# Router logits on four column tiles, a 128-column first gather, filler products and a new order of early expert loads in a two-layer decoder trunk

## The chip, the cores and the metric

The kernel runs on one core of one Trainium2 chip. The metric is the device time of one execution in microseconds; the median of three runs stands for it. Traces come from one profiled execution. The engines are called PE (matrix products, with PEld its weight loads), DVE (vector), ACT (scalar and activation), POOL and SP (whose queue issues nearly all loads here).

## The reference, cut to what matters

Two layers of a decoder trunk over 256 tokens of width 1024, all in float32. Each layer is an attention-like mixer followed by a channel mixer, each with RMSNorm before and after. The channel mixer of the second layer is a mixture of 8 experts, of which each token uses 2:

```python
logits = h @ w_router + b_router            # (256, 8)
probs = softmax(logits); top_p, top_e = top_k(probs, 2)
...
y = swiglu(rows, w_gate[e], w_up[e], w_down[e])   # 1024 -> 3584 -> 1024, per expert
out = segment_sum(y[dest] * sorted_w[:, None], sorted_tok)
```

The three matrices of an expert are 44 MB, those of all eight 352 MB; they are read once from HBM. The change lies at the border between the mixer of the second layer and these experts.

## The kernel before, in words

**Mixer, end of layer 1.** `mixer` ends with `wout(0, ...)`: products with `w_out` (L195 to L197, each float32 product as three of rounded parts) into accumulators, for token tile t = 0 and then t = 1 (128 tokens each). `update` scales, squares and adds the result to `self.x` (L401, L402, L408) and `measure` squares the new `x` (L245).

**Router logits.** `scorer` makes `ws` (router weights times the norm's scale, 8 columns for each of 8 slices of 128 channels). Its `score(t, after)` runs for t = 0 inside the update of t = 1 (behind an `Exp` on ACT) and for t = 1 after it. For each half of 512 channels it turns four 128x128 blocks of `x` on PE (L853, bank tag "s"), copies them to `xT` (L856 by ACT for t = 0; L858 by ACT and L859 by DVE, half each, for t = 1) and multiplies with the turned block as the weights and `ws` as 8 moving columns (L862): 8 products for each t.

**Routing.** `route` finishes the logits (L876), picks two experts per token by comparisons on DVE (L880 to L887), counts places with two products (L891, L892), and leaves `weights` for later. `places` makes the 0/1 matrix `pmr` (L1119), and `gather` multiplies `x` by it (L1139: 16 products of `x` blocks as weights with 64 moving columns for the first expert, which the profile counts as 32 instructions), scales the result (L1144 DVE, L1146 ACT), and the first expert's gate products (L1041) follow.

**Experts.** They run in a fixed order; four take 64 rows ("few": L1041, float32, two column tiles of 64) and four 128 rows (three products of rounded parts, L195 to L197, with conversions L179 on ACT and L180 on DVE). Expert 0 of the order is always the first one of the model, so its weights can be loaded before the routing is known. All weights are cut in units of 1 MB (42 per expert, 336 in all), loaded in the order of use by the generator `stream`; `take` hands them out.

**Where the early units go.** The first 18 units have a written `plan` of buffers: `None` is one of 6 rotating buffers `raw`, shared with the mixer's own loads and outside the expert pool; "g", "y", "f", "t4" are tiles of later use, taken as two halves of 512 KB; "a8" is one tag with 8 buffers of 1 MB. From unit 18 on, a `ring` of 15 buffers is used over again. SP's queue takes its issues in order; an issue whose buffer is still in use blocks those behind it. `behind` fixes the order of issue on one engine, and is no wait for the end of the other instruction.

The expert pool opens where the mixer's pools lay. Worked out from the shapes in the code, per partition and in order of address: "g" and "y" (8 KB each) lie on constants of the mixer and its `bias`; "f", "t4" on `os`, `on` and the rest of tag "h8"; then the eight 8 KB buffers, called a0 to a7 here: a0 on the tag "t2" (`xT` among it), a1 on its last buffer, `vv` and half of `kT`, a2 on `kT`, `qT`, `qn`, a3 on `qn`, `ks`, `vs`, `gr`, `gs`, a4 on small tiles and `sbe`, a5 on `sbe` and `sqs`, a6 on `sqs`, `gm` and `ws`, a7 beyond everything of the mixer of layer 1.

Of the kernel before, what the change touches and what calls it, by code (L numbers as in the profile page):

```python
# [9 lines left out]
F32 = mybir.dt.float32  # L10
# [5 lines left out]
OP = mybir.AluOpType  # L16
# [4 lines left out]
P = 128  # L21
D = 1024
S = 256
L = 2
KT = D // P
FF = 2816
FE = 3584
E = 8
EPS = 1e-6
BIG = 1e30  # L30
U = 2048
# [29 lines left out]
class Kernel:  # L61
# [6 lines left out]
    def run(self):  # L68
        tc, nc = self.tc, self.nc
        with ExitStack() as ctx:  # L70
            pool = lambda n, b, **k: ctx.enter_context(tc.tile_pool(name=n, bufs=b, **k))
            self.const = pool("const", 1)
            self.small = pool("small", 2)
            self.raw = pool("raw", RAW)
            self.hl = pool("hl", 4)
            self.psum = pool("psum", 2, space=PSUM)
            self.dr = pool("dr", 1, space=DRAM)
            with tc.tile_pool(name="mixers", bufs=1, reuse_waits="tile") as self.mix:
                with tc.tile_pool(name="set", bufs=1, reuse_waits="tile") as st:
# [746 lines left out]
    def level(self, l):  # L826
# [8 lines left out]
        nc.vector.tensor_tensor(level, pc[:, 0:E], self.brow, op=OP.add)  # L835
        return level

    def scorer(self, l, ph, ss, level):

        nc = self.nc  # L840
        wr = self.sm[:, SM_WR:SM_WR + 64].rearrange("p (k e) -> p k e", k=8)
        ws = ph.tile([P, KT, E], F32, name="ws")
        nc.vector.tensor_tensor(ws, wr, ss[:, :, None].to_broadcast([P, KT, E]), op=OP.mult)
        logits = []

        def score(t, after):
            pl = self.bank("t", "logits")
            logits.append(pl)
            for h in range(2):
                p = self.bank("s", "xT").rearrange("p (k t) -> p k t", k=4)  # L850
                xT = ph.tile([P, 4, P], F32, name="xT", tag="t2")
                for i in range(4):
                    nc.tensor.transpose(p[:, i], self.x[:, t, P * (4 * h + i):P * (4 * h + i) + P], self.ident)  # L853
                with self.behind(*after):
                    if t == 0:
                        nc.scalar.activation(xT, p, AF.Copy)  # L856
                    else:
                        nc.scalar.activation(xT[:, 0:2], p[:, 0:2], AF.Copy)  # L858
                        nc.vector.tensor_copy(xT[:, 2:4], p[:, 2:4])  # L859
                for i in range(4):  # L860
                    k = 4 * h + i
                    nc.tensor.matmul(pl[:, 0:E], lhsT=xT[:, i], rhs=ws[:, k], start=k == 0, stop=k == KT - 1)  # L862

        self.scores = logits, level
        return score

    def route(self, ph, gt, eq):


        nc = self.nc  # L870
        new = lambda n, *s: ph.tile([P, 2, *s], F32, name=n)
        pr, wt, pos, sel, scl = (new(n, E) for n in ("pr", "wt", "pos", "sel", "scl"))
        logits, level = self.scores
# [11 lines left out]
        selb = ph.tile([P, 2 * E], BF16, name="selb")  # L885
# [3 lines left out]
            nc.vector.tensor_scalar(scl[:, t], sel[:, t], r, None, op0=OP.mult)  # L889
        pp = self.bank("o", "places")  # L890
        nc.tensor.matmul(pp[:, 0:2 * E], lhsT=self.before, rhs=selb, start=True, stop=False, skip_group_check=True)  # L891
        nc.tensor.matmul(pp[:, E:2 * E], lhsT=self.one, rhs=selb[:, 0:E], start=False, stop=True, skip_group_check=True)  # L892
        nc.vector.tensor_copy(pos, pp[:, 0:2 * E].rearrange("p (t e) -> p t e", t=2))

        def weights():
# [52 lines left out]
    def moe(self, l, ph):  # L948
        tc, nc = self.tc, self.nc
        nch = FE // 512  # L950
        made = {}
# [2 lines left out]

        def tiles(tag):

            return made.get(tag) or [ph.tile([P, U // 2], F32, name="unit", tag=tag) for h in range(2)]

        def stream():

            last = ()
            plan = [None, None, None, "g", None, None, None, "y", "f", "t4", "a8", "a8", "a8", "a8", "a8", "a8", "a8", "a8"]
            ring = [t for t in plan if t in (None, "t4", "a8")]
            turn = 0
            for i, (name, p, u) in enumerate(units):
                tag = plan[i] if i < len(plan) else ring[(i - len(plan)) % len(ring)]
                if p == 0:
                    src = self.ins[name][FIRST, u]
                else:
                    if p > turn:  # L970
                        turn = p
                        expert.append(nc.values_load(turni[0:1, rank[p]:rank[p] + 1], engines=[ET.SP], min_val=0, max_val=E - 1))
                    src = self.ins[name][bass.ds(expert[p], 1), u].rearrange("o p f -> (o p) f")
                if tag is None:
                    yield self.load(src, after=last if i >= len(plan) else ())
                    if i > len(plan):
                        last = self.loaded,
                elif tag == "a8":
                    unit = ph.tile([P, U], F32, name="unit", tag=tag)
                    with self.behind(*(last if i >= len(plan) else ())):  # L980
                        self.loaded = nc.sync.dma_start(unit, src).ins
                    last = self.loaded,
                    yield unit
                else:
                    src = src.rearrange("p (h f) -> h p f", h=2)
                    unit = tiles(tag)
                    with self.behind(*(last if i >= len(plan) else ())):
                        for h, t in enumerate(unit):
                            self.loaded = nc.sync.dma_start(t, src[h]).ins
                    last = self.loaded,  # L990
                    yield unit
# [9 lines left out]
        ahead = [next(fetch) for i in range(4)]  # L1001
# [5 lines left out]
        made["f"] = tiles("f")  # L1007
        made["t4"] = tiles("t4")
        gm = ph.tile([P, D], F32, name="gm")
        ahead += [next(fetch) for i in range(14)]  # L1010
        made.clear()
        ss, sh = self.ffn_in
        wt, pos, sel, scl, weights = self.route(ph, gt, eq)

# [107 lines left out]
        def gather(e, pm, pmr, tags="t", xf=None):  # L1122

            few = short[e]
            n = 64 if few else P
            if few:
                xf = xf or ph.tile([P, KT, 64], F32, name="xf", bufs=2)
            else:
                xgh, xgl = [ph.tile([P, KT, P], F32R, name=n, tag="x4") for n in ("xgh", "xgl")]
            for h in range(2):  # L1130
                p = self.bank(tags[h % len(tags)], "gather").rearrange("p (a s) -> p a s", a=4)
                if not few:
                    xg = ph.tile([P, 4, P], F32, name="xg", tag="t2")
                else:
                    xg = xf[:, 4 * h:4 * h + 4]
                for a in range(4):
                    k = 4 * h + a
                    for t in range(2):
                        nc.tensor.matmul(p[:, a, 0:n], lhsT=self.x[:, t, P * k:P * k + P], rhs=pmr[:, t, 0:n],  # L1139
                                         start=a == 0 and t == 0, stop=t == 1, skip_group_check=True)  # L1140
# [52 lines left out]
        f, begun = [], None  # L1193
        for e in range(E):
# [3 lines left out]
            for c in range(nch):  # L1198
                pp = []
# [219 lines left out]
```

## Time and profile before

| what | value |
|---|---|
| median of 3 runs | 1452.79 us (1452.57 to 1456.24) |
| profiled execution, time | 1452.78 us |
| profiled execution, span | 1451.0 us, mean granted clock 0.968 |
| PE, DVE, ACT busy | 95%, 67%, 53% of the span |
| read from HBM | 479.87 MB, 332 GB/s over the span |
| DMA from 600 us on | about 420 GB/s until 1225 us |

The profiled execution's time is 1.8 us over its span, and as good as equal to the median, so sums can be made against it. Times in the rows below are microseconds from the start of the span. In the view by windows the numbers are the stretch, its length, the busy time (and count of instructions) of PE, PEld, DVE, ACT and POOL, the clock granted to PE as a share of full speed, the DMA share and GB/s. In the chain, each row is a start, a duration and the work that the end of the program goes back to. A busy PE is not one at its peak: records of products overlap, and their own durations (0.39 us for 512 columns) are longer than their distance (0.21 to 0.23 us).

### The profile page before, as it was taken

The numbers are of one execution on the slowest core, as the hardware profiler recorded it, in microseconds if no ns is written. First come the engines' busy times: TensorE is split into PE (matmuls) and PEld (weight loads), VectorE is DVE, ScalarE is ACT, GpSimd is POOL, SyncE is SP. The second block draws the span as 40 slices with busy tenths as digits, with TensorE's granted clock in tenths as the row PEclk, the third lists the DMA queues.
The fourth block names the chain that finished last, engine by engine and source line by source line (L and its number), as shares of the span: only waits on it lengthen the run. The fifth ranks groups of instructions, "written<-read, shape, count | busy, mean of one in ns | idle before, by whom it ended". The sixth has DMA issues, their size and how long they took to land.

```text
span 1451.0 us, 20370 instructions
## 1 busy us (share of the span) xinstructions
PE 1379.9 (95%) x7470; PEld 988.8 (68%) x7470; DVE 977.9 (67%) x1566; ACT 770.0 (53%) x1179; POOL 16.5 (1%) x24
## 2 busy tenths in 40 slices
PE   5899969999979999999999999999999999999996
PEld 5767759999877687544788534887435888788432
DVE  7678888877565774522999424998315989999413
ACT  3464654444554556232787324787324778787322
POOL 0100010000100000000000000000000000000000
PEclk9989979999979999799999999999999999999998
DMA  9936829888435284899999999999999999999994
GB/s 365 326 143 210 337 82 344 316 309 315 176 119 203 88 319 132 353 400 420 419 421 420 419 419 420 420 420 421 418 421 420 420 420 407 345 368 375 369 421 182
DMA packets 73479, 482.52 MB, mean 333 GB/s; under 512 B 10315, under 2 KB 10484, under 8 KB 18588
## 3 DMA queue, kind: packets, MB, share of 16 engines
q1 hardware_dynamic: 72876, 479.91, 83.7%
q0 software_dynamic: 496, 1.25, 0.4%
q8 instruction: 60, 0.98, 0.3%
q14 instruction: 47, 0.39, 0.1%
HBM read 479.87 MB, written 1.25 MB: 332 GB/s over the span
## 4 chain that ended last, share of the span: by engine, by line
PE 64%; DVE 3%; ACT 1%; issue 1%; DVEq 0%; ACTq 0%
PE moe_gate L1041 7%; PE moe_up L1041 7%; PE yacc L1041 7%; PE moe_gate L196 4%; PE moe_gate L195 4%; PE moe_gate L197 4%; PE yacc L196 3%; PE yacc L195 3%; PE yacc L197 3%; PE moe_up L196 3%; PE moe_up L197 3%; PE moe_up L195 3%; PE gT L1099 2%; PE gather L1177 1%; DVE wlo L180 1%; PE po L618 1%
## 5 line engine op out<-in xcount | busy, mean ns | idle before, releaser
L179 ACT ACTIVATE whi<-raw 128x1024 fp32r<-128x1024 f32 x260 | 271.7, 1058 | 162.6 <-PE ffn_gate L196 33.0
L180 DVE TENSOR_TENSOR wlo<-raw,whi 128x1024 fp32r<-128x1024 f32 x256 | 307.0, 1223 | 74.1 <-ACT whi L179 68.8
L180 DVE TENSOR_TENSOR wlo<-unit,whi 128x1024 fp32r<-128x1024 f32 x202 | 236.7, 1221 | 9.3 <-ACT whi L179 5.4
L179 ACT ACTIVATE whi<-unit 128x1024 fp32r<-128x1024 f32 x202 | 208.4, 1057 | 34.0 <-PE moe_up L197 16.1
L207 DVE CUSTOM_DVE_ANT_0 raw<-raw,cb,sm 128x1024 f32<-128x1024 f32 x96 | 120.7, 1279 | 3.1 <-DMA raw<-in_w_ada_dram 3.1
L1089 DVE TENSOR_TENSOR sg<-moe_gate,sg 64x512 f32<-64x512 f32 x28 | 19.1, 681 | 113.5 <-ACT sg L1088 113.5
L196 PE MATMUL moe_up<-wlo,xgh 128*128 128x512 f32 x224 | 88.6, 395 | 3.9 <-DVE wlo L180 3.9
L196 PE MATMUL yacc<-wlo,g 128*128 128x512 f32 x224 | 89.3, 399 | 0.3 <-DVE wlo L180 0.3
L195 PE MATMUL moe_gate<-whi,xgh 128*128 128x512 f32 x224 | 88.2, 394 | 0.0
L195 PE MATMUL yacc<-whi,g 128*128 128x512 f32 x224 | 88.0, 393 | 0.0
L196 PE MATMUL moe_gate<-wlo,xgh 128*128 128x512 f32 x224 | 87.9, 392 | 0.0
L195 PE MATMUL moe_up<-whi,xgh 128*128 128x512 f32 x224 | 87.7, 392 | 0.0
L197 PE MATMUL yacc<-whi,g 128*128 128x512 f32 x224 | 87.4, 390 | 0.0
L197 PE MATMUL moe_up<-whi,xgl 128*128 128x512 f32 x224 | 87.4, 390 | 0.0
L197 PE MATMUL moe_gate<-whi,xgl 128*128 128x512 f32 x224 | 87.4, 390 | 0.0
L1089 DVE TENSOR_TENSOR up<-moe_up,up 64x512 f32<-64x512 f32 x28 | 19.1, 683 | 72.7 <-ACT up L1088 72.7
L1041 PE MATMUL moe_up<-unit,xf 128*64 128x512 f32 x288 | 66.3, 596 | 0.0
L1041 PE MATMUL yacc<-unit,gf 128*64 128x512 f32 x272 | 62.2, 593 | 0.0
L1041 PE MATMUL moe_gate<-unit,xf 128*64 128x512 f32 x240 | 57.1, 598 | 0.0
L1088 ACT ACTIVATE sg<-moe_gate 64x512 f32<-64x512 f32 x28 | 16.6, 594 | 72.6 <-PE moe_gate L1041 72.6
L195 PE MATMUL ffn_gate<-hh,whi 128*128 128x256 f32 x176 | 51.2, 291 | 2.5 <-ACT hh L315 2.4
L196 PEld LDWEIGHTS moe_up<-wlo,xgh 128*128 128x128 f32 x224 | 42.0, 188 | 16.6 <-DVE wlo L180 8.2
(410 smaller groups left out, 2926.1 us busy)
## 6 DMA issues: line engine op xcount, KB each, us to landing
unit<-in_moe_gate_dram SPq DMA_DIRECT2D x66, 1024.0 KB, 14.9
unit<-in_moe_up_dram SPq DMA_DIRECT2D x56, 1024.0 KB, 14.6
unit<-in_moe_down_dram SPq DMA_DIRECT2D x54, 1024.0 KB, 16.1
raw<-in_w_ada_dram SPq DMA_DIRECT2D x48, 1024.0 KB, 6.5
raw<-in_moe_gate_dram SPq DMA_DIRECT2D x46, 1024.0 KB, 14.5
raw<-in_moe_down_dram SPq DMA_DIRECT2D x45, 1024.0 KB, 15.6
raw<-in_moe_up_dram SPq DMA_DIRECT2D x44, 1024.0 KB, 13.7
raw<-in_w_in_dram SPq DMA_DIRECT2D x16, 1024.0 KB, 5.8
```

The costliest lines, as they stand in the source:

```text
L179: self.last_hi = nc.scalar.activation(hi, w, AF.Copy)
L180: last_lo = (nc.gpsimd if self.count < 2 else nc.vector).tensor_sub(lo, w, hi.bitcast(F32))
L195: nc.tensor.matmul(out, lhsT=ahi, rhs=bhi, start=first, stop=False, skip_group_check=True)
L196: nc.tensor.matmul(out, lhsT=ahi, rhs=blo, start=False, stop=False, skip_group_check=True)
L197: nc.tensor.matmul(out, lhsT=alo, rhs=bhi, start=False, stop=last, skip_group_check=True)
L207: self.nc.vector.tensor_tensor_reduce(w[:, j], w[:, j], self.cb, 1.0, self.sm[:, b:b + 1], OP.mult, OP.add, self.modc[:, l, o:o + 1])
L618: nc.tensor.matmul(po[64 * g:64 * g + 64, :], lhsT=lhs, rhs=rhs, start=first[g], stop=last, skip_group_check=True)
L1041: m = nc.tensor.matmul(out[64 * kk:64 * kk + 64], lhsT=x[:, k], rhs=w[:, 512 * kk:512 * kk + 512], start=first and h == 0, stop=last and h ...
L1088: nc.scalar.activation(to, p[64:128], AF.Copy)
L1089: nc.vector.tensor_add(to, p[0:64], to)
L1099: nc.tensor.transpose(tr[0][:, j, 0:n], sg[0:n, P * j:P * j + P], self.ident[0:n, 0:n])
L1177: nc.tensor.matmul(p[:, a], lhsT=self.x[:, t, P * k:P * k + P], rhs=both[:, t], start=a == 0 and t == 0, stop=t == 1, skip_group_check=True)
```

## The change

Five edits. (1) `ws` is padded to 32 columns with zeros (a memset on POOL). In `score` the four products of a half now have `ws` as weights and the turned block as 128 moving columns, each into its own strip of 32 partitions; two halves accumulate, and `total` copies the 128x128 block to SBUF (`part`, DVE) and adds the four strips by a product with `self.sel`. `total` of t = 0 is called at the start of `score(1)`, that of t = 1 at its end. (2) `idle(n, after)` issues n bfloat16 products of 512 columns into a bank of tag "p" that nothing reads, behind a given product: 6 after the turns of t = 0, 4 after those of t = 1, 7 after the total of t = 1, 2 after the places. (3) The gather uses all 128 columns of `pmr` for experts with 64 rows too. (4) The 8 early buffers get a tag of their own each, and the plan is a7, a3, six `raw`, "g", "y", a2, a4, a1, a5, a0, a6, "f", "t4". (5) The first 18 issues are tied to this order, and all are made after the pool's tiles are laid out.

```diff
-                self.moe(L - 1, Phase(ph, t4=2, t2=3, x4=2, f=2, y=2, g=2, a8=8))
+                self.moe(L - 1, Phase(ph, t4=2, t2=3, x4=2, f=2, y=2, g=2, **{f"a{i}": 1 for i in range(8)}))
...
+    def idle(self, n, after):
+
+        warm = self.bank("p", "warm")
+        with self.behind(after):
+            for i in range(n):
+                self.nc.tensor.matmul(warm.rearrange("p (a t) -> p a t", a=4), lhsT=self.one,
+                                      rhs=self.one[:, None].to_broadcast([P, 4, P]), start=True, stop=True)
...
-        ws = ph.tile([P, KT, E], F32, name="ws")
-        nc.vector.tensor_tensor(ws, wr, ss[:, :, None].to_broadcast([P, KT, E]), op=OP.mult)
+        ws = ph.tile([P, KT, 32], F32, name="ws")
+        nc.gpsimd.memset(ws, 0.0)
+        nc.vector.tensor_tensor(ws[:, :, 0:E], wr, ss[:, :, None].to_broadcast([P, KT, E]), op=OP.mult)
...
-            logits.append(pl)
+            logits.append(pl[:, 2 * P:3 * P])
+            if t:
+                self.total(after)
...
+                if h:
+                    self.idle(6 - 2 * t, last.ins)
...
-                    nc.tensor.matmul(pl[:, 0:E], lhsT=xT[:, i], rhs=ws[:, k], start=k == 0, stop=k == KT - 1)
+                    nc.tensor.matmul(pl[32 * i:32 * i + 32, 0:P], lhsT=ws[:, 4 * h + i], rhs=xT[:, i], start=h == 0, stop=h == 1,
+                                     skip_group_check=True)
+
+            def total(after):
+                part = ph.tile([P, P], F32, name="part", bufs=2)
+                with self.behind(*after):
+                    nc.vector.tensor_copy(part, pl[:, 0:P])
+                return nc.tensor.matmul(pl[:, 2 * P:2 * P + E], lhsT=part, rhs=self.sel[:, 0:E], start=True, stop=True,
+                                        skip_group_check=True)
+
+            if t == 0:
+                self.total = total
+            else:
+                self.idle(7, total(after).ins)
...
+        self.idle(2, last.ins)
         nc.vector.tensor_copy(pos, pp[:, 0:2 * E].rearrange("p (t e) -> p t e", t=2))
...
-            plan = [None, None, None, "g", None, None, None, "y", "f", "t4", "a8", "a8", "a8", "a8", "a8", "a8", "a8", "a8"]
-            ring = [t for t in plan if t in (None, "t4", "a8")]
+            plan = ["a7", "a3", None, None, None, None, None, None, "g", "y", "a2", "a4", "a1", "a5", "a0", "a6", "f", "t4"]
+            ring = [t for t in plan if t not in ("g", "y", "f")]
...
-                    yield self.load(src, after=last if i >= len(plan) else ())
-                    if i > len(plan):
-                        last = self.loaded,
+                    unit = self.load(src, after=last)
+                    last = self.loaded,
+                    yield unit
...
-                        nc.tensor.matmul(p[:, a, 0:n], lhsT=self.x[:, t, P * k:P * k + P], rhs=pmr[:, t, 0:n],
+                        nc.tensor.matmul(p[:, a], lhsT=self.x[:, t, P * k:P * k + P], rhs=pmr[:, t],
                                          start=a == 0 and t == 0, stop=t == 1, skip_group_check=True)
```

More of the change, by code (lines that the diff above doesn't have):

```diff
@@ L852, in score @@
                 for i in range(4):
-                    nc.tensor.transpose(p[:, i], self.x[:, t, P * (4 * h + i):P * (4 * h + i) + P], self.ident)
+                    last = nc.tensor.transpose(p[:, i], self.x[:, t, P * (4 * h + i):P * (4 * h + i) + P], self.ident)
+                if h:
+                    self.idle(6 - 2 * t, last.ins)
                 with self.behind(*after):
@@ L860, in score @@
                 for i in range(4):
-                    k = 4 * h + i
-                    nc.tensor.matmul(pl[:, 0:E], lhsT=xT[:, i], rhs=ws[:, k], start=k == 0, stop=k == KT - 1)
+                    nc.tensor.matmul(pl[32 * i:32 * i + 32, 0:P], lhsT=ws[:, 4 * h + i], rhs=xT[:, i], start=h == 0, stop=h == 1,
[10 more added lines that the diff above has]
+                self.idle(7, total(after).ins)
         self.scores = logits, level
@@ L891, in route @@
         nc.tensor.matmul(pp[:, 0:2 * E], lhsT=self.before, rhs=selb, start=True, stop=False, skip_group_check=True)
-        nc.tensor.matmul(pp[:, E:2 * E], lhsT=self.one, rhs=selb[:, 0:E], start=False, stop=True, skip_group_check=True)
+        last = nc.tensor.matmul(pp[:, E:2 * E], lhsT=self.one, rhs=selb[:, 0:E], start=False, stop=True, skip_group_check=True)
+        self.idle(2, last.ins)
         nc.vector.tensor_copy(pos, pp[:, 0:2 * E].rearrange("p (t e) -> p t e", t=2))
@@ L955, in tiles @@
         def tiles(tag):
-            return made.get(tag) or [ph.tile([P, U // 2], F32, name="unit", tag=tag) for h in range(2)]
+            return made.pop(tag, None) or [ph.tile([P, U // 2], F32, name="unit", tag=tag) for h in range(2)]
         def stream():
             last = ()
-            plan = [None, None, None, "g", None, None, None, "y", "f", "t4", "a8", "a8", "a8", "a8", "a8", "a8", "a8", "a8"]
-            ring = [t for t in plan if t in (None, "t4", "a8")]
+            plan = ["a7", "a3", None, None, None, None, None, None, "g", "y", "a2", "a4", "a1", "a5", "a0", "a6", "f", "t4"]
+            ring = [t for t in plan if t not in ("g", "y", "f")]
             turn = 0
@@ L974, in stream @@
                 if tag is None:
-                    yield self.load(src, after=last if i >= len(plan) else ())
-                    if i > len(plan):
-                        last = self.loaded,
-                elif tag == "a8":
-                    unit = ph.tile([P, U], F32, name="unit", tag=tag)
-                    with self.behind(*(last if i >= len(plan) else ())):
+                    unit = self.load(src, after=last)
+                    last = self.loaded,
+                    yield unit
+                elif tag[0] == "a":
+                    unit = made.pop(tag, None) or ph.tile([P, U], F32, name="unit", tag=tag)
+                    with self.behind(*last):
                         self.loaded = nc.sync.dma_start(unit, src).ins
@@ L986, in stream @@
                     unit = tiles(tag)
-                    with self.behind(*(last if i >= len(plan) else ())):
+                    with self.behind(*last):
                         for h, t in enumerate(unit):
@@ L1000, in moe @@
         fetch = stream()
-        ahead = [next(fetch) for i in range(4)]
+        made["g"] = tiles("g")
         made["y"] = tiles("y")
@@ L1009, in moe @@
         gm = ph.tile([P, D], F32, name="gm")
-        ahead += [next(fetch) for i in range(14)]
-        made.clear()
+        for i in range(8):
+            made[f"a{i}"] = ph.tile([P, U], F32, name="unit", tag=f"a{i}")
+        ahead = [next(fetch) for i in range(18)]
         ss, sh = self.ffn_in
```

## The prediction

> **What bounds the kernel now.** I read the waits of PE first, for everything after the border (590 us to the end):
>
> ```profile
> PE moe_up L196 <- DVE wlo L180: 3.9, 8, 0.6
> PE places L891 <- DVE selb L886: 1.9, 1, 1.9
> ...
> PE gather L1139 <- DVE pmr L1119: 0.8, 1, 0.8
> ```
>
> The largest sum is 3.9 us in 860, and none of the nine rows of that answer names a DMA. So the experts are a PE-bound stretch: what PE gains before its first expert product it should keep to the end, as long as the loads stay ahead of it. Next the chain of work that ended last, across the border:
>
> ```profile
> 579.32 0.49 ACT xT L856
> 579.86 3.37 PE logits L862 x16
> 583.22 1.80 PE xT L853 x8
> 585.02 3.23 PE logits L862 x16
> 588.28 0.24 DVE pr L876
> ...
> 591.12 1.11 PE gather L1139 x4
> 592.24 6.07 PE gather L1139 x28
> 598.32 4.74 PE moe_gate L1041 x16
> 607.01 3.43 PE moe_gate L1041 x16
> ```
>
> Some 23 us pass between the last `x` and full expert work, and 19 of them are PE rows that look too long: 16 gate products take 4.74 us first and 3.43 us later. The view by windows, cut where the clock changes, says why (stretch, length, busy time of five engines, clock, DMA share, GB/s):
>
> ```profile
> 576.71:580.12 3.41, 1.56 (x13) 1.20 (x12) 3.23 (x14) 3.31 (x12) 0.00 (x0) 1.00 0.51 136
> 580.12:583.53 3.41, 3.41 (x18) 3.41 (x18) 1.85 (x6) 1.56 (x5) 0.00 (x0) 0.50 1.00 390
> ...
> 593.77:597.19 3.42, 3.42 (x18) 3.42 (x18) 0.34 (x1) 0.81 (x2) 0.00 (x0) 0.50 1.01 422
> 597.19:600.60 3.41, 3.41 (x13) 1.74 (x14) 2.14 (x14) 0.81 (x2) 0.00 (x0) 0.50 1.01 425
> 600.60:604.01 3.41, 3.41 (x18) 1.10 (x16) 2.09 (x14) 0.85 (x2) 0.00 (x0) 1.00 1.01 425
> ```
>
> After a window in which PE worked 1.56 of 3.41 us, the granted clock is 0.50 for six windows, 20.5 us: logits, turns, gather and the first gate products all run at half clock. A window full of 64-column gathers (593.77) didn't end it, one with 512-column gate products (597.19) did. So what counts seems to be columns that stream, not PE being busy.
>
> **The change, part by part.** Durations of what it touches:
>
> ```profile
> 579.86 3.37 PE L862 MATMUL logits<-ws,xT 128*128 128x8 f32 x16 [1.85 <-ACT xT L856]
> 580.16 1.42 DVE L408 SCALAR_TENSOR_TENSOR x<-m,rur,x 128x512 f32<-128x512 f32 x2
> 581.61 0.63 ACT L245 ACTIVATE scr<-x 128x512 bf16<-128x512 f32 x1
> 585.06 0.38 ACT L858 ACTIVATE xT<-xT 128x256 f32<-128x256 f32 x1 [0.47 <-PE xT L853]
> 585.48 0.42 DVE L859 COPY xT<-xT 128x256 f32<-128x256 f32 x1 [0.43 <-ACT xT L858]
> 1172.74 3.73 PE L1139 MATMUL gather<-pmr,x 128*128 128x128 f32 x32
> ```
>
> ```profile
> L573 PE MATMUL cmp<-raw,cb 128*32 128x256 f32 x64 | 4.9, 384 | 0.0
> L491 PE MATMUL pg<-sel,gT x8: 266/266/287, 66.3 to 446.0; 64*128 64x24 f32 x8
> ```
>
> *Logits of t = 0.* Before, they hold PE until 583.22, though the second `x` is ready at 580.16 + 1.42 = 581.58. L573 is the same form as the new products (four strips of 32, fp32): 64 instructions of 256 columns in 4.9 us, so 16 with half the columns lie between 0.6 and 1.2 us. PE is free by about 581 and the turns of t = 1 follow `x` by 581.6 to 582.2. The copies are then bound by ACT: the square L245 must go first (581.61 + 0.63 and its readout of 0.19 partly beside it, so 582.33).
>
> *Logits of t = 1.* ACT and DVE copy a half in turn (the row of L859 waits for L858): 582.33 + 0.38 + 0.03 + 0.42 = 583.2, the second half's DVE part until 583.6. Products of the last half by L573: 0.3 to 0.6, so 584.1. The copy to `part` has no row; between the 0.42 us of 256 columns from PSUM and 0.17 us of tiny copies I take 0.3: 584.4. The total is two instructions of the kind of L491, a weight load of 0.19 and 0.27 us: 584.9 with the hand-over. `pr` starts at 584.95 in place of 588.28: **-3.3 us**. From `pr` to the gather nothing is removed: 591.12 - 588.28 = 2.84 us stay.
>
> *Gather.* 591.12 to 598.3, 7.2 us at half clock, against 3.57 to 3.73 us for 32 instructions of twice the columns at full clock: **-3.6 us**. The width itself costs nothing there: with 128 columns an instruction takes 0.112 us, and the 64-column ones took 0.217 us at half clock, 0.109 at full; the load of 128 weight columns is what sets the distance.
>
> *First gate products.* 4.74 us for the first sixteen, 3.43 us in the row at 607.01 and up to 3.58 us in others of the kind: **-1.2 us**.
>
> *Idle products.* Nineteen, by the distance of 512-column products in the expert stage (0.21 to 0.23 us) 4.0 to 4.4 us of PE. Their cover: six (1.4 us) in PE's wait of 1.85 us for `xT` (578.01 to 579.86); four (0.9 us) between the turns' end (582.2) and the copies' (583.2); seven (1.6 us) in the 1.86 us from `pr` to the places, the 1.9 us row above; two (0.45 us) in the wait for `pmr`, 0.8 us. Cost nothing at full clock. If the cover is gone, that is at half clock, seven take 3.0 us and push the places by 1.1 us. Their bank of tag "p" was last read by the update of t = 1 before 578.0, so no new wait.
>
> *`total` of t = 0.* Its copy queues on DVE behind L408 (581.58) and its product can stand on PE ahead of the turns of t = 1, which are then late until 582.3: 0 to 1.2 us on the path. I take the middle, **+0.6 us**. *Memset and wider `ws`*: POOL is 1% busy and `ws` is needed only at 579.9; nothing.
>
> *Loads.* SP's rows around the border, and the ACT row that first reads the last two units:
>
> ```profile
> 529.10 3.88 SPq L167 DMA_DIRECT2D raw<-in_moe_gate_dram  x2
> ...
> 563.64 2.00 SPq L989 DMA_DIRECT2D unit<-in_moe_up_dram  x4
> 577.17 1.86 SPq L989 DMA_DIRECT2D unit<-in_moe_down_dram  x4
> 588.27 0.80 SPq L981 DMA_DIRECT2D unit<-in_moe_gate_dram  x2
> ...
> 654.69 1.98 SPq L981 DMA_DIRECT2D unit<-in_moe_gate_dram  x2
> ...
> 676.80 3.89 ACT L179 ACTIVATE whi<-unit 128x1024 fp32r<-128x1024 f32 x4
> ```
>
> Ten units are issued by 578.5, then nothing until the logits end at 588.27, since the eight buffers begin with the one on `xT`. From there on DMA runs at 420 GB/s, 2.5 us a unit, and PE eats a unit of the first expert in 1.8 us, so the lead melts until the second expert: its first units are issued at 654.69 and 656.3, take 14.9 us by the page's median, somewhat more while eight are in flight, and are first read at 676.8 and 678.7. The spare is 5 to 7 us, less than the 7.5 us that I forecast for PE. So the new order must pay in. By the layout, a7 is free throughout, a3 after the last use of `vs` (506.5 to 507.6 in the trace), the six `raw` as before, a2, a4, a1, a5 when the stick-breaking attention is done (565 to 568). That makes 14 units instead of 10 issued by 568, and the last four (a0, a6, "f", "t4") at about 584.5, when logits and total are read, instead of 588.27: 4 x 2.5 + 3.8, some 14 us more lead. Spare 5 + 14 - 7.5 = 11 us at the second expert: enough. Later, DMA falls to 376 to 379 GB/s between 1200 and 1400 us because buffers are full, so nothing is short there. SP's new order puts a7 and a3 ahead of the expert's `raw` loads, not of the mixer's.
>
> **The sum.** -3.3 - 3.6 - 1.2 + 0.6 = -7.5 us against the profiled execution's 1452.8 us (span 1451.0 and 1.8 us around it; as good as the median): **1445.3 us**. All of it hangs on the clock. What lets it fall? Two stretches at full clock, by form, each with the window that followed it:
>
> ```profile
> L746 PE MATMUL sbo<-sbe,vv 128*64 128x256 f32 x4 | 1.3, 404 | 0.0
> L761 PE MATMUL ssb<-ones,sqs 128*128 128x1 f32 x7 | 1.1, 256 | 0.0
> L387 PE MATMUL rows<-ident,gc 128*128 128x128 f32 x5 | 1.0, 289 | 0.0
> L749 PE MATMUL sbo<-sbe,vv 128*64 128x128 f32 x4 | 0.8, 285 | 0.0
> ...
> 566.47:569.88 3.41, 3.41 (x23) 3.06 (x23) 1.31 (x7) 1.69 (x5) 0.00 (x0) 1.00 0.95 298
> ```
>
> ```profile
> L672 PE MATMUL qc<-kcT,qn 64*128 64x7 f32 x16 | 2.1, 255 | 0.0
> L195 PE MATMUL pq<-hh,whi 128*128 128x256 f32 x4 | 1.3, 322 | 0.0
> ...
> 467.48:470.90 3.42, 3.42 (x16) 2.40 (x16) 2.60 (x15) 0.11 (x2) 0.00 (x0) 0.50 0.00 0
> ```
>
> The first (563.05 to 566.47) kept the full clock, the second (464.07 to 467.48) lost it. With 128 fp32 columns at 0.107 us (0.112 above less a little issue), half that where two strips share the array, the first streams 0.43 + 0.53 + 0.21 and three rows of `z` of 0.32, together 1.5 us or 44%; the second eleven `pq` of 0.107 (four in the row, seven more of L196 and L197) and almost nothing else, 1.2 us or 36%. The window that lost the clock at 580.12 has eight turns, three logits and the last two `wo`, about 1.3 us or 38%. So the bound lies near 40%, 1.4 us of a window. In the new order the thinnest 3.41 us begin when the first six idle products end (579.4): products 0.4, turns 0.85, half of the next idle products 0.6, together 1.9 us or 55%; every other position holds more. The clock should stay.
>
> [...]
>
> **The rivals.**
>
> *The clock falls all the same* (turns or strip products count less than I think). Then: turns of t = 1 until 583.0, four idle products until 584.7, last products 585.9, total 587.0; seven idle products until 590.0 hold the places, gather from 591.0, now dense enough to end the half clock a window earlier. Gain 1 to 3.5 us: 1449.3 to 1452, say 1450.5. For it: three thin gaps remain. Against it: the 55%. [...]
>
> *The loads don't move ahead* (they stay near 588 as the `a8` loads did, a7 and a3 included, though these buffers were free). Then PE's gain beyond the spare of 5 to 7 us turns into a wait for a load at the second expert: 1452.8 - 5 = 1447.8.
>
> *Slower: the tied order stalls SP.* If a7 or a3 waits for more than its own tile (a pool's end, say), the six `raw` behind it, at 529 to 556 now, wait too. PE is then short of loads once fewer than 8 units have been issued where 10 were. If all stand until 585, the 42nd unit lands at 585 + 2.5 + 42 x 2.5 = 692.5, 21 us after 678.7 - 7.5: 1452.8 - 7.5 + 21 = 1466.5. For it: a7 and a3 sat free in the kernel before and were not loaded early. Against it: "g" was issued at 563.64 within the mixer, so waits go by tile.
>
> *It does nothing*, PE's chain being bound by DVE and ACT at both clocks: 1452.8. The four PE rows above speak against it.
>
> **How the numbers follow.** Forecast 0.64 (own range 1443 to 1447.5: copy, total and order of `total` at either bound), clock falls 0.14, loads don't move 0.10, stall 0.07, nothing 0.05. A change under 0.3% (4.4 us, up from 1448.4) cannot be told from none here. Faster: 0.64 + 0.10 + 0.02 of the clock case = 0.76; same 0.12 + 0.05 = 0.17; slower 0.07. The range reaches down to 1443 and up to 1451, where most of the clock case lies; stall and nothing stay out.
>
> **What would show it.** Clock 1.00 in all windows from 576 to 604; gather of 32 in 3.6 us; `pr` of t = 1 some 3.3 us nearer to L408; SP issues of a7 and a3 before 529 and four more by 568, no PE wait for a DMA near 670. I am wrong if a 0.50 stands there, if PE's rows of waits name loads, or if the mixer's own loads come later than now.

## The result, and the profile after

| kernel | median | range | runs |
|---|---|---|---|
| before | 1452.79 us | 1452.57 to 1456.24 | 5 |
| changed | 1444.61 us | 1440.84 to 1446.57 | 5 |

The ratio is 0.9934 (95% interval 0.9916 to 0.9952), 8.2 us less; 1445.3 was forecast. A second comparison, told below, gave 0.9939 (0.9917 to 0.9961). The profiled execution took 1446.57 us, span 1444.8, mean granted clock 0.973 against 0.968. The number came out, but the traces show that it is not the sum that was forecast: the border gave what was expected, a gain in the experts was not foreseen, and a chance loss ahead of the border hid it in this profile.

PE at the border in the changed kernel (start, duration, line, names, shapes, count, and in brackets the idle time before it and what ended it):

```profile
582.41 1.03 PE L864 MATMUL xT<-ident,x 128*128 128x128 f32 x8
583.28 1.46 PE L843 MATMUL warm<-one 128*128 128x512 bf16 x6
585.40 0.82 PE L874 MATMUL logits<-xT,ws 128*32 128x128 f32 x16 [0.67 <-ACT xT L869]
586.51 1.18 PE L864 MATMUL xT<-ident,x 128*128 128x128 f32 x7 [0.28 <-DVE x L408]
587.52 0.29 PE L881 MATMUL logits<-sel,part 128*128 128x8 f32 x2
587.67 0.31 PE L864 MATMUL xT<-ident,x 128*128 128x128 f32 x1
...
590.24 0.39 PE L881 MATMUL logits<-sel,part 128*128 128x8 f32 x2 [0.39 <-DVE part L880]
590.48 1.67 PE L843 MATMUL warm<-one 128*128 128x512 bf16 x7
592.53 0.17 PE L916 MATMUL places<-selb,before 128*128 128x16 bf16 x1 [0.38 <-DVE selb L911]
...
593.51 3.84 PE L1166 MATMUL gather<-pmr,x 128*128 128x128 f32 x32 [0.34 <-DVE pmr L1146]
...
597.31 3.65 PE L1068 MATMUL moe_gate<-unit,xf 128*64 128x512 f32 x16
600.90 0.44 PE L1187 MATMUL pmT<-ident,pm 128*128 128x128 f32 x2
```

The gather is 3.84 us instead of 7.2, the first sixteen gate products 3.65 instead of 4.74 in the forecast's row. On DVE:

```profile
585.61 1.41 DVE L408 SCALAR_TENSOR_TENSOR x<-m,rur,x 128x512 f32<-128x512 f32 x2
...
589.89 0.29 DVE L880 COPY part<-logits 128x128 f32<-128x128 f32 x1 [0.64 <-PE logits L874]
...
590.67 0.23 DVE L901 SCALAR_TENSOR_TENSOR pr<-logits,rnr,level 128x8 f32<-128x8 f32 x1 [0.35 <-PE logits L881]
```

From the last `x` (L408) to `pr` it takes 5.06 us; before it was 588.28 - 580.16 = 8.12. The granted clock is 1.00 from 503.7 us to 1435.5, some 9 us ahead of the end. By windows, three stretches across the border (columns as in the prediction; the clock's own windows, 3.41 us each by its records, begin 1.05 us later):

```profile
581.15:584.57 3.42, 3.42 (x21) 2.31 (x19) 3.31 (x11) 3.32 (x12) 0.00 (x0) 1.00 0.33 139
584.57:587.98 3.41, 2.42 (x28) 1.52 (x28) 2.86 (x11) 2.76 (x8) 0.00 (x0) 1.00 0.32 48
587.98:591.39 3.41, 3.02 (x27) 1.38 (x26) 2.30 (x11) 0.80 (x4) 0.00 (x0) 1.00 1.01 423
```

**Where the time lies.** The same instructions can be compared by their start in two traces. Three ACT instructions cut the program: one just ahead of the last `wo` products, one behind the border, one near the end. First the kernel before, then the changed one, then a second profile of the changed one:

```profile
565.94 0.38 ACT L752 ACTIVATE sqs<-sbo 128x256 f32<-128x256 f32 x1 [1.80 <-PE sbo L749]
647.65 0.38 ACT L1103 ACTIVATE gf<-gT 128x256 f32<-128x256 f32 x1 [3.28 <-PE gT L1099]
1423.22 0.59 ACT L1088 ACTIVATE sg<-moe_gate 64x512 f32<-64x512 f32 x1 [3.15 <-PE moe_gate L1041]
```

```profile
571.39 0.38 ACT L752 ACTIVATE sqs<-sbo 128x256 f32<-128x256 f32 x1 [1.80 <-PE sbo L749]
645.56 0.38 ACT L1130 ACTIVATE gf<-gT 128x256 f32<-128x256 f32 x1 [3.28 <-PE gT L1126]
1417.40 0.59 ACT L1115 ACTIVATE sg<-moe_gate 64x512 f32<-64x512 f32 x1 [3.15 <-PE moe_gate L1068]
```

```profile
563.50 0.38 ACT L752 ACTIVATE sqs<-sbo 128x256 f32<-128x256 f32 x1 [1.80 <-PE sbo L749]
637.66 0.38 ACT L1130 ACTIVATE gf<-gT 128x256 f32<-128x256 f32 x1 [3.28 <-PE gT L1126]
1409.60 0.59 ACT L1115 ACTIVATE sg<-moe_gate 64x512 f32<-64x512 f32 x1 [3.15 <-PE moe_gate L1068]
```

Against before, the changed kernel is 5.45 us late ahead of the border, then 2.09 early, then 5.82 early: border -7.54, experts -3.73. In the second profile it is 2.44 early, 9.99, 13.62: border -7.55, experts -3.63. The parts behind `wo` agree to 0.1 us; the part ahead of it, where no code was changed, differs by 7.9 us. The table gives the same three differences for every run (the kernels are described below), from all matched ACT and DVE instructions near these points (microseconds against the one profile of before; ratio of times with its interval):

| kernel | ahead | border | experts | ratio |
|---|---|---|---|---|
| changed | +5.4 | -7.55 | -3.7 | 0.9934 (0.9916 to 0.9952) |
| changed, again | -2.4 | -7.55 | -3.6 | 0.9939 (0.9917 to 0.9961) |
| PE side alone | +5.5 | -7.55 | +0.1 | 0.9961 (0.9946 to 0.9976) |
| loads alone | -0.5 | -1.31 | -3.7 | 0.9976 (0.9957 to 0.9995) |
| no idle products | +0.7 | -4.69 | -3.7 | 0.9937 (0.9916 to 0.9958) |
| turns as idle products | -0.4 | -7.18 | -3.7 | 0.9936 (0.9914 to 0.9959) |
| old logits | +2.8 | -7.52 | -3.6 | 0.9944 (0.9923 to 0.9964) |
| old ring | +3.3 | -7.54 | +11.1 | 1.0022 (1.0008 to 1.0036) |
| ring turned | -2.3 | -7.54 | +0.7 | 0.9953 (0.9937 to 0.9969) |
| idle products at all borders | +3.4 | -7.44 | -3.8 | 0.9930 (0.9906 to 0.9954) |
| PE side, t4 last | +1.8 | -7.54 | -3.7 | 0.9946 (0.9924 to 0.9968) |
| two edits | +0.3 | -7.56 | -3.5 | 0.9945 (0.9927 to 0.9964) |
| two edits, all borders | +0.6 | -7.54 | -3.4 | 0.9937 (0.9913 to 0.9961) |

In the two kernels with idle products at all borders the first column holds what these did as well; in the first of them it is read at 573 us, and at the row of 565.94 it is +2.0. The parts separate what the times can't: one execution's lead-in varies more than any two of the faster kernels differ.

### The profile page after: what moved, and what is told of

It reads as the page before. It is cut to its first block, busy times and chain, and to the rows that moved or that the text cites. A ratio compares the mean times of both kernels' runs of the same rounds, so it can differ in the third digit from the quotient of the medians.

```text
span 1444.8 us, 20430 instructions
## 1 busy us (share of the span) xinstructions
PE 1376.1 (95%) x7493; PEld 985.2 (68%) x7493; DVE 979.9 (68%) x1568; ACT 771.3 (53%) x1179; POOL 16.8 (1%) x25
## 4 chain that ended last, share of the span: by engine, by line
PE 64%; DVE 4%; ACT 1%; issue 1%; DVEq 0%; ACTq 0%
PE moe_gate L1068 7%; PE moe_up L1068 7%; PE yacc L1068 7%; PE moe_gate L195 4%; PE moe_gate L196 4%; PE moe_gate L197 4%; PE yacc L195 4%; PE yacc L196 3%; PE yacc L197 3%; PE moe_up L196 3%; PE moe_up L197 3%; PE moe_up L195 3%; PE gT L1126 2%; DVE wlo L180 1%; PE gather L1204 1%
## 5 line engine op out<-in xcount | busy, mean ns | idle before, releaser
L179 ACT ACTIVATE whi<-raw 128x1024 fp32r<-128x1024 f32 x260 | 271.3, 1057 | 166.8 <-PE ffn_gate L196 33.2
L179 ACT ACTIVATE whi<-unit 128x1024 fp32r<-128x1024 f32 x202 | 210.7, 1058 | 38.5 <-PE moe_gate L197 16.9
L1068 PE MATMUL yacc<-unit,gf 128*64 128x512 f32 x296 | 66.9, 593 | 0.5 <-ACT gf L1130 0.5
L1068 PE MATMUL moe_gate<-unit,xf 128*64 128x512 f32 x264 | 64.2, 599 | 0.0
L1068 PE MATMUL moe_up<-unit,xf 128*64 128x512 f32 x256 | 58.9, 596 | 0.0
```

The source lines that it names most:

```text
L179: self.last_hi = nc.scalar.activation(hi, w, AF.Copy)
L1068: m = nc.tensor.matmul(out[64 * kk:64 * kk + 64], lhsT=x[:, k], rhs=w[:, 512 * kk:512 * kk + 512], start=first and h == 0, stop=last and h ...
```

## The experiments

**The PE side alone.** The load plan, ring and ties are those of before.

```diff
-            plan = ["a7", "a3", None, ..., "g", "y", "a2", "a4", "a1", "a5", "a0", "a6", "f", "t4"]
+            plan = [None, None, None, "g", None, None, None, "y", "f", "t4", "a8", ...]
```

> The tiled logits, the idle products and the 128-column gather of the changed kernel, with the expert loads in the old plan (eight a8 buffers at the end). My theory: the border still gains 7.5 us (last wo to first pmT 18.8 us, clock 1.00 throughout), but PE then reaches the second expert with less spare than the 5 to 7 us it had, so a wait of PE or ACT for a unit of 0.5 to 2.5 us shows near 665 to 690 us, and the time is 1446 to 1449. Rival A (loads were never short): no such wait, the time equals the changed kernel's, 1444.6. Rival B (the experts' 3.7 us beyond the border come from the order of loads): the shift against the kernel before stays at -7.5 us from the border to the end, without the later -3.7.

The border gained its 7.55 us, and no wait for a load came: the largest of PE's waits in the experts is 4.0 us for `wlo`, none names a DMA. My theory that the spare would run out here fell. The experts stood flat at +0.1: the 3.7 us belong to the plan of the loads.

**The loads alone.** The kernel before with the plan, ring, ties and buffers of the changed one; logits, gather and products as before, and no idle products.

```diff
-            plan = [None, None, None, "g", None, None, None, "y", "f", "t4", "a8", ...]
-            ring = [t for t in plan if t in (None, "t4", "a8")]
+            plan = ["a7", "a3", None, None, None, None, None, None, "g", "y", "a2", "a4", "a1", "a5", "a0", "a6", "f", "t4"]
+            ring = [t for t in plan if t not in ("g", "y", "f")]
```

> The new plan and order of the expert loads alone; logits, gather and PE order as before, no idle products. My theory: the clock falls to 0.50 for some 20 us at the border as before, PE's chain is the old one, and the time is within 0.3% of the kernel before (1449 to 1456). Rival B (the experts' 3.7 us beyond the border come from the order of loads): 1449, with the gain between 770 and 1360 us. Rival C (the tied order stalls SP): slower, with PE waits that name a DMA.

Rival B was right: experts -3.7 us. The clock fell to 0.50 from 582.7 to 599.7, 17.0 us and not 20.5: the windows lay otherwise to the work and one fewer was slow. The border's -1.31 fits that, as chance and not as an effect of the loads; no run parts the two.

**No idle products.**

```diff
     def idle(self, n, after):
+        return
```

> The changed kernel without any of its nineteen idle products. My theory (a window of 3.41 us has to stream about 40% of its columns): windows between the last wo and the places hold under 1.2 us of streaming, so the clock is 0.50 for four to six windows from about 585 us; logits 0.3 us slower, gather 7.2 us in place of 3.8 or a part of it: 1447 to 1451. Rival D (the tiled products and the wider gather are dense enough, the idle products do nothing): clock 1.00, the time of the changed kernel, 1444.6.

By windows, and the PE rows behind it:

```profile
577.28:580.69 3.41, 1.46 (x15) 1.12 (x17) 3.23 (x14) 3.31 (x12) 0.00 (x0) 1.00 0.01 5
580.69:584.10 3.41, 3.35 (x30) 2.46 (x33) 2.49 (x8) 2.00 (x7) 0.00 (x0) 0.51 0.48 137
584.10:587.52 3.42, 1.54 (x18) 0.62 (x13) 2.56 (x13) 0.69 (x3) 0.00 (x0) 0.99 1.00 422
587.52:590.93 3.41, 2.04 (x11) 1.98 (x11) 2.63 (x14) 0.21 (x1) 0.00 (x0) 0.51 0.91 300
590.93:594.34 3.41, 3.41 (x18) 3.41 (x18) 0.34 (x1) 0.63 (x2) 0.00 (x0) 0.50 1.00 413
```

```profile
589.08 6.34 PE L1167 MATMUL gather<-pmr,x 128*128 128x128 f32 x32 [0.88 <-DVE pmr L1147]
...
595.38 3.65 PE L1069 MATMUL moe_gate<-unit,xf 128*64 128x512 f32 x16
```

The clock falls twice, as the theory said, and comes back between, in a window of turns and strip products at half clock. The gather runs at half clock for most of its 6.34 us, but with 128 columns it ends the drop (the clock is 0.99 from 594.34 us) before the gate products. The idle products are worth 7.55 - 4.69 = 2.9 us here; strips and width saved the rest without them. The forecast of 1447 to 1451 missed (1442.94): the 3.7 us of the experts weren't in it, and three windows were at half clock, not four to six.

**Turns as idle products.** Each product of 512 columns becomes two fp32 turns.

```diff
-                self.nc.tensor.matmul(warm..., lhsT=self.one, rhs=..., start=True, stop=True)
+                for j in range(2):
+                    self.nc.tensor.transpose(warm[:, P * j:P * j + P], self.slots, self.ident)
```

> The changed kernel with each idle product (one product of 512 columns) replaced by two fp32 turns (transposes) of a 128x128 constant, about the same time of PE. My theory (turns count for the clock like products): clock 1.00 through the border, the time of the changed kernel, 1444.6 +- 1. [...]

```profile
576.28:579.69 3.41, 2.77 (x27) 2.43 (x29) 3.23 (x14) 3.31 (x12) 0.00 (x0) 1.00 0.02 7
579.69:583.11 3.42, 3.10 (x36) 2.05 (x32) 2.89 (x10) 2.59 (x9) 0.00 (x0) 1.00 0.62 170
583.11:586.52 3.41, 3.00 (x31) 2.24 (x31) 1.99 (x12) 0.00 (x0) 0.00 (x0) 1.00 1.01 425
```

The clock stays at 1.00 through windows in which about four fifths of the columns that stream are turns: counted from the forms of the instructions, everything else makes 10 to 12% of a window there, and without any idle products it fell (to 0.51 from 580.69 us). In the changed kernel a window whose only products were thirteen turns (408.1 to 411.5 us) also raised the clock, from 0.50 to 1.00. These fp32 turns count.

**Old logits.** The changed kernel with 8-column products as before, idle products kept.

```diff
-                    nc.tensor.matmul(pl[32 * i:32 * i + 32, 0:P], lhsT=ws[:, 4 * h + i], rhs=xT[:, i], ...)
+                    last = nc.tensor.matmul(pl[:, 0:E], lhsT=xT[:, i], rhs=ws[:, k], start=k == 0, stop=k == KT - 1)
```

> The changed kernel with the old form of the logits (turned x blocks as weights, 8 moving columns, 16 products per token tile, no copy and no sum of strips); idle products, wide gather and loads as changed. My theory: the clock stays 1.00 (turns and idle products stream 43% or more of each window), the 16 instructions of t = 1 take 1.7 us in place of 3.4 at half clock, and pr of t = 1 comes 0 to 1 us later than in the changed kernel: total +0 to +1 us, so most of the 3.1 us gained between L408 and pr came from the clock, not from the strips. Rival: logits of 8 columns stream so little that a window falls under 40%: 0.50 for some windows, border 3 to 5 us longer than in the changed kernel.

Border -7.52: equal. With the full clock held, L408 to `pr` is 588.01 - 582.94 = 5.07 us with the old logits, 5.06 with the strips. In this profile the strips save nothing that the clock doesn't. What they may add is reserve, and that is counted below.

**Old ring.** From unit 18 on the buffers are reused in the old rotation.

```diff
-            ring = [t for t in plan if t not in ("g", "y", "f")]
+            ring = [None] * 6 + ["t4", "a7", "a3", "a2", "a4", "a1", "a5", "a0", "a6"]
```

> The changed kernel with one line different: from unit 18 on, the 15 buffers are reused in the old rotation (six raw first, then t4, then the eight a buffers) in place of the order of the plan. The first 18 loads, their order and buffers stay. In the compiled program the order of PE instructions in the experts is then that of the kernel before: 61 groups of gT turns and 18 of scatter products, against 57 and 16. My theory (the experts' 3.7 us are the order of instructions, set when the program is built, and not earlier data): border -7.5 us as in the changed kernel, and the 3.7 us are gone: flat shift from 612 us to the end, as in the kernel with the PE side alone. Rival F (the units that come earlier make it): the 3.7 us stay.

The experts lost 11.1 us, all of it between 660 and 700 us, and are flat from there on: without the 3.7. What was lost is a shortage that I hadn't foreseen. SP's issues from 608 us on, and PE's waits from 612 to 720:

```profile
608.52 2.04 SPq L167 DMA_DIRECT2D raw<-in_moe_gate_dram  x2
635.26 1.19 SPq L1015 DMA_DIRECT2D unit<-in_moe_up_dram  x2
```

```profile
PE moe_up L1068 <- DMA raw<-in_moe_up_dram: 2.0, 2, 1.6
PE moe_gate L195 <- ACT whi L179: 2.0, 1, 2.0
...
PE moe_gate L1068 <- DMA raw<-in_moe_gate_dram: 0.7, 2, 0.6
```

Unit 24 goes into `t4`, which in this plan holds unit 17, read shortly before 635: SP stands for 24.7 us, and the eight issues behind it then go within 7 us. Here buffers had to come round in the order in which they were first filled. Since the loads were late too, this run alone could not exclude rival F.

**PE side, t4 last.** This run does.

```diff
-            plan = [None, None, None, "g", None, None, None, "y", "f", "t4", "a8", ... "a8"]
+            plan = [None, None, None, "g", None, None, None, "y", "f", "a8", ... "a8", "t4"]
```

> The kernel with the PE side alone (old plan of loads, the last eight not issued before about 590 us), with one name moved: t4 stands last in the plan in place of tenth. So the buffer that is loaded in two halves comes at units 32, 47, 62 and so on, as in the changed kernel, and not at 24, 39, 54. In the compiled program the order of PE instructions in the experts is then exactly that of the changed kernel; the early loads stay late. My theory (the 3.7 us are that order): border -7.5 us and experts another -3.7 us against the kernel before, as in the changed kernel. Rival F (they come from data that is there earlier): border alone, flat after 612 us.

Experts -3.7 us with the early loads as late as before, one of them later. The rival falls: it is the order of PE's instructions, which follows from where the buffer in two halves comes in the ring. All fourteen traces agree. Behind the first gather, PE's instructions stand in one of three orders. The first has 61 groups of `gT` turns and 18 of scatter products: before, the PE side alone and the old ring, none of which has the 3.7 us. The second has 57 and 16, in ten kernels, and all ten gained 3.4 to 3.8 us. The third, 56 and 15, is that of the next run. What the order does can be seen at one place. First the PE side alone, then this kernel (rows of the three-part products left out):

```profile
806.54 0.73 PE L1094 MATMUL scatter<-y,pmTs 128*128 128x512 f32 x2 [0.46 <-ACT y L1086]
808.48 0.63 PE L1094 MATMUL scatter<-y,pmTs 128*128 128x512 f32 x2
810.19 1.94 PE L1067 MATMUL moe_up<-unit,xf 128*64 128x512 f32 x8
```

```profile
804.47 1.10 PE L1094 MATMUL scatter<-y,pmTs 128*128 128x512 f32 x4
805.50 1.94 PE L1067 MATMUL moe_up<-unit,xf 128*64 128x512 f32 x8
```

In the first, two scatter products are put where PE must wait 0.46 us for their `y`; in the second all four stand together behind it. An ACT instruction behind this place (L1114, `up`) starts at 815.17 and 810.48, 4.7 us apart, one ahead of it (L179) at 769.81 and 765.88, 3.9 apart: the place is worth 0.8 us. It comes again near 1356, the split `rows` turns near 1079 are worth 0.9, and smaller steps lie near 768, 990, 1110 and 1135.

**Ring turned.** Chosen since its program has the fewest split groups.

```diff
+            ring = ring[4:] + ring[:4]
```

> The changed kernel with the ring of 15 buffers started at its fifth place (three raw, a2, a4, ...). In the compiled program all 56 groups of gT hold four turns and the scatter products stand in 15 groups, fewer than in the changed kernel (57 and 16). Theory of the order of instructions: another 0.3 to 1.5 us less in the experts than the changed kernel, steps at places where groups were split. Rival: units 22 to 28 wait for buffers read only 12 units before, and PE shows waits for loads near 650 us: slower by up to 3 us.

```profile
ACT whi L179 <- DMA unit<-in_moe_gate_dram: 3.9, 3, 2.6
ACT whi L179 <- DMA raw<-in_moe_gate_dram: 3.0, 2, 2.6
```

These are ACT's waits in the experts. The rival was right on the wait, and it comes twice (674 and 883 us), 1.7 us on PE each time; a further 1.0 us against the changed kernel is lost near 1079, where the `rows` turns are split 2 and 6. Fewer groups is no measure of a better order.

**Two edits.** The kernel before with idle products, and t4 last; all else as it was.

```diff
-            plan = [None, None, None, "g", None, None, None, "y", "f", "t4", "a8", ... "a8"]
+            plan = [None, None, None, "g", None, None, None, "y", "f", "a8", ... "a8", "t4"]
...
+                if h:
+                    self.idle(6 - 2 * t, last.ins)
...
+            if t:
+                self.idle(7, last.ins)
...
+        self.idle(2, last.ins)
```

> The kernel before with two edits only: the nineteen idle products (6 behind the turns of t = 0, 4 behind those of t = 1, 7 behind the last logits, 2 behind the places) and t4 last in the old plan. Logits in their old form, 64-column first gather, early loads late. My theory (the clock and the order of the experts' instructions are all of the gain): clock 1.00 through the border, gather of 32 in 3.6 to 3.9 us with 64 columns, border -7.5, experts -3.7, the time of the changed kernel. Rival: the 64-column gather streams too little and the clock falls in it: border -4 us or less.

```profile
588.39 0.66 PE L1152 MATMUL gather<-pmr,x 128*128 128x64 f32 x4 [0.34 <-DVE pmr L1132]
...
588.91 3.32 PE L1152 MATMUL gather<-pmr,x 128*128 128x64 f32 x28
...
592.16 3.65 PE L1054 MATMUL moe_gate<-raw,xf 128*64 128x512 f32 x16
```

Border -7.56, experts -3.5; the 64-column gather takes 588.39 to 592.2, 3.8 us, as the wide one. In this profile nineteen idle products and one name moved bring the gain of all five edits to within 0.2 us. This kernel and the changed one can't be told apart by their times (0.9945 and 0.9939, each +-0.002).

**The changed kernel again.**

> The changed kernel once more, for a narrower interval beside the others. By its parts (border -7.5, experts -3.7, nothing changed before) it should be 11 us under the kernel before, ratio 0.992 to 0.993; in the first profile 5.4 us of that were lost in the mixer of layer 0, which has the same code. If that loss belongs to the change it shows again in the profile: +5 us by 160 us; if it is the chance position of the clock's windows, another value between -2 and +6 us.

Its lead-in was 2.4 us shorter than that of before, not 5.4 longer. The early loss of the first profile is not the change.

**Idle products at the borders of the first layer.** In the changed kernel, and then in the one with two edits:

```diff
+        if l == 0:
+            self.idle(34, self.last_mm.ins, "s")
...
+        self.idle(24, self.last_mm.ins, "s")
...
+                if t and h:
+                    self.idle(8, turn.ins, "t")
```

> The changed kernel with idle products at the other two borders of the trunk as well: 34 behind the last wo product of the first mixer, 24 behind the last down product of the first channel mixer, 8 behind the last turns of the norm after each. In the changed kernel the clock is 0.50 from 199.9 to 217.0 and from 404.7 to 421.8 us. My theory: these stretches disappear; the chains there are on DVE and ACT until 210.5 and 415.3, so only what follows gains, some 3.2 us each (6.5 us of products at half clock), and about 1 us of turns: 6 to 8 us less than the changed kernel, 1437 to 1439. Rival: the idle products hold up turns and products that wait behind them on PE: under 3 us or slower.

> The kernel with the two edits alone (idle products at the border, t4 last in the plan), and idle products at the two borders of the first layer as well (34, 24, 8 and 8). In the run with them in the changed kernel these borders gained 0.9 and 2.4 us, and 2.6 us were lost again in half-clock windows of the second mixer. If that loss was the chance position of windows: 3 us less than the kernel with the two edits; if fuller windows ahead bring thinner ones later: no gain over it.

The second of these borders by one window of 17 us, in the changed kernel and with the added products:

```profile
405.00:422.00 17.00, 10.22 (x47) 9.31 (x47) 12.90 (x34) 10.89 (x24) 0.22 (x1) 0.61 0.29 78
```

```profile
405.00:422.00 17.00, 12.81 (x94) 10.65 (x93) 13.56 (x28) 11.66 (x24) 0.00 (x0) 1.00 0.30 110
```

The clock rises from 0.61 to 1.00, and the borders gain 0.9 and 2.4 us (1.0 and 2.4 in the second kernel), not the 6 to 8 that I worked out; DVE and ACT seem to carry most of these chains. The first of these gains isn't clear of chance: the PE side alone gained 0.8 us at that border without such products, and three other kernels 0.5. The second mixer then lost 2.5 us in one run and gained 1.5 in the other, with half-clock windows at other places. Both times stay within the intervals of the kernels without these products (medians 1444.17 and 1441.52): whether this beats the changed kernel is open.

## Why the prediction was right, and where it was not

*The clock: right.* It stays at 1.00 at the border with idle products, falls to 0.50 without them, and turns count. Counted over all fourteen traces in one way (fp32 columns twice, since in the changed kernel the 128 of a turn take 0.109 us and the 512 bfloat16 ones of an idle product 0.216; strips by their share of the array, since four of their products start within 0.02 us; an instruction to the window in which it starts), from 150 us on and without the program's last 40 us: of 63 windows that lost the clock 61 had at most 37.1% of their columns, of some 5000 that kept it all but two had at least 37.5%. The four exceptions are in the two kernels with idle products in the first layer. So the forecast's bound near 40% was a little high. In the first 150 us windows of up to 75% lost it all the same, which this count doesn't explain.

*Its margin: wrong.* The forecast gave the thinnest 3.41 us of the border 55%, and every other position more. By the count above, taken at every position, the thinnest stretch of the changed kernel (from 584.4 us) holds 37.9%: sixteen instructions of strip products, eight turns and a sum of strips, and no idle product. So by this count the clock is held wherever the windows fall, but by little. In the kernels with the old logits and with two edits, windows in 44 to 47% of all positions would meet a stretch under 37.3%, down to 22 and 25%. Their profiles didn't meet one, and kept the clock. This is an estimate from the three traces, and no run tests it: strips and wide gather may still buy that such a kernel never loses the clock here.

A fall of the clock would have cost less than the rival said: 2.9 us of the border, as the run without idle products shows, for strips and wide gather hold their part then. Two sums of the forecast are off, without weight: the rows given as 19 us add up to 20.3, and 1452.8 - 7.5 + 21 is 1466.3.

*Logits -3.3, gather -3.6, first gate products -1.2: right, each 0.1 to 0.2 too large.* Measured: 8.12 - 5.06 = 3.06, 7.2 - 3.8 = 3.4, 4.74 - 3.65 = 1.1; together 7.55, all of the border. The copy to `part` took 0.29 us where I took 0.3.

*`total` of t = 0, +0.6: wrong, about zero.* It did stand between the turns (the rows at 587.52 and 587.67), but behind seven of the eight, with 0.15 us. The two misses cancel in the sum by luck.

*What makes the logits faster: half right.* I put -3.3 down to the strips and the clock together without parting them. With the clock held, strips and old logits give the same; without idle products, the strips bring L408 to `pr` from 8.12 to 5.33 us (580.82 to 586.15 in that run). The clock had come back at 584.10 there, so how much the strips save at half clock is not shown.

*The loads: wrong.* Not 14 units by 568 but 12 by 574 (568.6 without the 5.45 us of lead-in), for a1 and a5 waited until 585.92; what held them is not shown:

```profile
533.71 0.90 SPq L1007 DMA_DIRECT2D unit<-in_moe_gate_dram  x2
...
571.19 2.90 SPq L1007 DMA_DIRECT2D unit<-in_moe_gate_dram  x2
585.92 0.81 SPq L1007 DMA_DIRECT2D unit<-in_moe_up_dram  x2
```

The step that failed is "the spare is 5 to 7 us, less than the 7.5": I let PE come earlier and left the last eight loads where they were, though they wait for the logits, which came 3 us earlier too. By the traces' landing times the spare of the second expert's second unit (issued 656.26, landed 673.61, read at 676.65 in the PE side alone) is 3.0 us without the new plan, 7.4 with it, 5.4 before. There the plan was insurance that nothing drew on. With t4 last in the old plan there was need of it: nine units then wait for the logits instead of eight, and the same unit lands at 672.79 and is read at 672.95 in the PE side with t4 last, a spare of 0.2 us. With two edits it is read as it lands (671.62, 671.64), and ACT waits for units in the experts, the longest near 880 and 1091 us:

```profile
ACT whi L179 <- DMA raw<-in_moe_gate_dram: 1.6, 2, 1.1
ACT whi L179 <- DMA unit<-in_moe_gate_dram: 1.5, 2, 1.0
```

In the changed kernel no such wait is longer than 0.3 us. The price is small, 0.1 to 0.4 us less gain in the experts of the two kernels with two edits. SP's queue didn't stall in the way that the rival feared: the mixer's last `w_out` loads, at 530.99, are ahead of a7 and a3.

*The experts: missing.* The sum held no term for them; it had taken the order of their instructions for given. That term was not in the prediction, and at -3.7 us it is half as large as the border. Border and experts make -11.2 us; the first comparison showed -8.2, the second -9.8 (1450.53 to 1440.78), for the lead-in differs from run to run by more than that gap. So the forecast of 1445.3 met 1444.6 by a right border, a missed gain and a chance loss.

## What to carry to other kernels

Where a chain of small dependent steps runs between two dense stages, look at the granted clock first: a few idle products in PE's waits gave here what tiled products and a wider gather gave only in part, and with them neither took any time off in these profiles. Count the thinnest stretch too, for the clock's windows lay otherwise to the work in each profile. Compare traces by stage, on matched instructions: stage differences repeated to 0.1 us where whole times scattered by 8. And when an edit moves a buffer, compare the order of instructions in stages it doesn't seem to touch, and let buffers be reused in the order of their first filling.

## What the runs showed of the hardware that I had not expected

The clock's windows lay otherwise to the work in each profile, and the lead-in went with how many of them were slow. Twelve profiles have the same code ahead of the border; it took from 2.4 us less to 5.5 us more than in the one of before. The clock's records have three to seven half-clock windows in the first 150 us of the seven that lay between -2.4 and +0.7, and eight to ten in the five between +1.8 and +5.5. That the windows' position decides this is argued from these counts; no run sets it. In the two profiles of the changed kernel the first record of the full clock stands at 12.18 and 24.72 us, 3.67 windows of 3.413 us apart: no whole number, so the windows of these two lay otherwise to the start of the span.
